# Adding residual rows and half of each attention output by accumulating transfers, and two gate tiles of their own, in a hybrid decoder block

## The chip, the cores and the metric

The kernel runs on one core of a Trainium2 chip. Its time is the device time of one execution in microseconds; the number that counts is the median of several executions. The core has TensorE (matrix products, written PE in the profile, its weight loads PEld), VectorE (DVE), ScalarE (ACT), GpSimd (POOL) and SyncE (SP). SP issues the transfers between DRAM and the on-chip memories.

## The reference

One decoder layer on x of 1024 rows by 1024 columns, all in float32, cut to what matters:

```
u = rmsnorm(x);  proj = u @ w_in                      # columns for both groups
ya = dilated_attention(q, k, v)                       # 8 heads x 64, causal, three dilated windows, merged softmax
yb = hgrn2(q, f, i): S_t = diag(f_t) S_(t-1) + (1 - f_t) i_t^T;  o_t = S_t^T q_t     # 4 heads x 128
yb = rmsnorm(o) * norm_w * silu(g)                    # g: the output gate
h  = x + concat(ya, yb) @ w_out                       # residual
h  = h + (silu(u2 @ w_gate) * (u2 @ w_up)) @ w_down,  u2 = rmsnorm(h)
out = rmsnorm(h)
```

## The kernel before

The whole kernel is a list of operations with costs, in program order, from which a scheduler in the kernel file writes out the order on each engine. `P.op` (and `P.flex`, for operations that may go to one of several engines) records an operation with its cost and the tiles that it reads and writes. `schedule` simulates the engines with these costs: an operation is ready when those that it depends on have ended, and among ready ones the class (`P.cls`, lower first) and then the longest remaining path decide. A transfer counts as landed 1.2 us after its issue (0.5 us), plus its bytes' time on a shared line (`moved`; 0.18 us for 64 KB), plus 0.97 us. At run time each engine takes its instructions in that order and waits on semaphores; it never passes a waiting instruction. Tiles are named by tag (`E0` to `E16`, `wh0`, `lm` and so on); a new tile with an old tag must wait until all uses of the old one have ended.

Matrix products are split in high and low float32r parts, three products for each; large ones use a Strassen scheme, so VectorE, ScalarE and POOL split, combine and evict.

The stages. First the input projection in twelve blocks of 256 or 512 columns; the last block is V. Its results go to DRAM (q_d, f_d, g_d, i_d, v_d and others). `hgrn(h)` runs the recurrence for heads 0 to 3 (class 0, the first to be picked), on the tiles E14 (f and the keys ks), E15 (q forms) and E16 (A, the score matrix, and iv, the values). It evicts scores to A on VectorE (lines 895 and 870), updates the state, forms o on TensorE from A and iv, normalises it and multiplies by the gate (line 958, recorded at L311 by `stt`). The gate g is loaded into A itself, `gt = A` (lines 945 and 946), after TensorE's last read of it. `attention(h, js)` (class 1) takes pairs of 128-row blocks: scores, masked maximum on VectorE (L1017, the mask `am` in E8), exponentials on ScalarE, scaling by the reciprocal (`wh<-wh,ri`) on POOL or VectorE, transposes (L1054), and the product with V. V is split in a high and a low part side by side in the weights, so the product has 128 rows: 64 of the high and 64 of the low part, which must be added. Two ScalarE copies (yb and ya in the tile `lm`), one add and one transfer bring 64 x 256 results to m_d in DRAM. The output projection (class 2, `out_proj`) fills TensorE's time in between: for each of eight row blocks t it first takes the recurrence rows 0 to 2 of the mixed matrix, later rows 3 to 7, and adds the product on VectorE to hn. hn starts as the rows of x, loaded beforehand into E13, E6, E15 and E16 by four transfers of 1 MB. Then come the norm, the gate/up products and the down product, in which TensorE is busy throughout.

Of the kernel before, what the change touches and what calls it, by code (L numbers as in the profile page):

```python
# [13 lines left out]
AF = mybir.ActivationFunctionType  # L14
OP = mybir.AluOpType
# [4 lines left out]
S = 1024  # L20
D = 1024
# [50 lines left out]
class Prog:  # L72
# [44 lines left out]
    class Clock:  # L117
# [7 lines left out]
        def to(self, t):  # L125
            while t >= (self.win + 1) * self.W:
                share = self.busy / self.W
                self.fast = share > 0.42 if self.fast else share > 0.84
                self.win, self.busy = self.win + 1, 0.0
# [123 lines left out]
def hymba_block(ctx: ExitStack, tc: tile.TileContext, x, norm1_w, w_in, lb_logits, hgrn_norm_w, w_out,  # L253
                norm2_w, w_gate_up, w_down, final_norm_w, cos, sin, amask, lmask, eye, out):
    nc = tc.nc
    x = x[0]
    out = out[0]
# [5 lines left out]
    P = Prog()  # L263
# [5 lines left out]
    def moved(nbytes, run):  # L269

        return nbytes / run * (0.008 + run / 27e3) / 16

    def dma(o, i, nbytes, run=2048):
        r = [i] if isinstance(i, (View, Buf)) else []
        w = [o] if isinstance(o, (View, Buf)) else []
        gi = i if r else (lambda: i)
        go = o if w else (lambda: o)
        P.op("SP", 0.5, lambda: nc.sync.dma_start(go(), gi()), r, w, nbytes=moved(nbytes, run))

    def mm(items, r, w):  # L280
        cost = sum(4 * n / 2400.0 + 0.008 if f32 else n / 2400.0 + (0.0132 if n > 128 else 0.007)
                   for o, lt, rh, st, sp, n, m, f32 in items)

        def fn():
            for o, lt, rh, st, sp, n, m, f32 in items:
                nc.tensor.matmul(o(), lt(), rh(), start=st, stop=sp, skip_group_check=True)  # L286
        P.op("PE", cost, fn, r, w)
# [9 lines left out]
    def bank_of(x):  # L297
        return (x.buf if isinstance(x, View) else x).pool == "ps"

    def two(n, psum=False):  # L300

        dve = ("DVE", 0.07 + n * 1.04e-3, not psum)
        return [dve] if psum else [dve, ("POOL", 0.17 + n * 2.1e-3, True)]

    def tt(eng, o, a, b, op, n, f=1.0):
        alts = two(n, bank_of(a) or bank_of(b) or bank_of(o) or op == OP.max)
        P.flex(alts, lambda e: ENG[e].tensor_tensor(o(), a(), b(), op=op), [a, b], [o])  # L307
# [16 lines left out]
    def act(o, a, func, n, scale=1.0, bias=None, accum=None):  # L324
        r, w, kw = [a], [o], {}
        cost = (0.06 if a.buf.pool == "ps" else 0.095) + n * 0.83e-3
        for k, s in (("scale", scale), ("bias", bias)):
            if isinstance(s, View):
                r.append(s)
                cost += 0.09  # L330
        if accum is not None:
            w.append(accum)
            cost += 0.09

        def fn():
            kw = {}
            if isinstance(scale, View) or scale != 1.0:
                kw["scale"] = scale() if isinstance(scale, View) else scale
            if bias is not None:
                kw["bias"] = bias()  # L340
            if accum is not None:
                kw["accum_out"] = accum()
            nc.scalar.activation(o(), a(), func, **kw)  # L343
        P.op("ACT", cost, fn, r, w, aset=SETS.get(func))
# [16 lines left out]
    whole = lambda b: b.v(lambda t: t)  # L361
# [9 lines left out]
    lm = P.buf("lm", [128, 10, 64], I32)  # L371
# [24 lines left out]
    def bank(stream, shape=(128, 512)):  # L396
        names = BANKS[stream]
        while True:
            n = rot[stream] = rot.get(stream, -1) + 1
            tag = f"b{names[n % len(names)]}"  # L400
            if tag not in held:
                return P.buf(tag, list(shape), F32, "ps")

    def turn(name, n):
        rot[name] = rot.get(name, -1) + 1
        return rot[name] % n
# [10 lines left out]
    def E(i, shape, dt=F32):  # L417
        return P.buf(f"E{i}", shape, dt)

    def colv(b, a, n, key):  # L420
        return b.v(lambda t: t[:, a:a + n], key)
# [10 lines left out]
    m_d = P.buf("m_d", [D, S], F32, "dr")  # L432
# [73 lines left out]
    def mm3(o, lh, ll, rh, rl, start, stop, n, m=128):  # L506
        return [(o, lh, rh, start, False, n, m, False), (o, lh, rl, False, False, n, m, False),
                (o, ll, rh, False, stop, n, m, False)]
# [321 lines left out]
    def hgrn(h):  # L830
        rs = slice(h * 128, h * 128 + 128)
        f, ks = colv(E14, 0, S, 0), colv(E14, S, S, 1)
        qp = colv(E15, 0, S, 0)
        A, iv = colv(E16, 0, S, 0), colv(E16, S, S, 1)
# [19 lines left out]
        def scores(n, g):  # L854

            ps = bank("h", (128, 2, 192))
            mm([(ps.v(lambda b, c=c: b[:, c, :n]), cs(ks, 2 * g + c),
                 E15.v(lambda t, c=c: t[:, S + (2 * g + c) * 192:S + (2 * g + c) * 192 + n]),
                 True, True, n, 128, True) for c in range(2)], [half(ks, g // 2), E15.v(None, 1)], [ps])
            return ps  # L860
# [31 lines left out]
        for g in range(4):  # L892
            ps = scores(192, g)
# [7 lines left out]
        for i, l in enumerate((1, 3, 5)):  # L901
# [8 lines left out]
            for g in range(4):  # L910
                ps = scores(192, g)
# [14 lines left out]
        for g in range(2):  # L926
            ps = bank("h")
# [9 lines left out]
        for c in range(NT):  # L937
            o = pj(po[c // 4], c % 4)
# [3 lines left out]
                it.append((o, cs(qp, c), cs(ks, c - 1), False, True, 128, 128, True))  # L942
                rd += [half(qp, c // 4), half(ks, (c - 1) // 4)]
            mm(it, rd, [o])
        gt = A
        dma(gt, g_d.v(lambda b: b[rs, :], h), 128 * S * 4)
        ss = P.buf("hss", [128, NT])
        for g in range(2):
# [10 lines left out]
            dma(m_d.v(lambda b, g=g: b[h * 128:h * 128 + 128, g * 512:g * 512 + 512], (h, g)), yg, 128 * 512 * 4)  # L959


    am = E(8, [128, 2048])
    ys = []
    amv = am.v(lambda t: t[:, :1920])
    EA = [[E(i, [128, 2048], F32R) for i in p] for p in ((9, 10), (11, 12))]
    probs = Ring(["wh4", "wh5", "wh6", "wh7", "wh8", "wh9", "wh10", "wh11"])
    PT = [("wl8", "wl9"), ("wl10", "wl11"), ("wl4", "wl5")]
# [19 lines left out]

    def attention(h, js):
        G = h // 4
        yb, ya = ys  # L990
        EQ, EV = EA[h % 2]
        qs, kh = colv(EQ, 0, S, 0), colv(EQ, S, S, 1)
        vv, kl = colv(EV, 0, S, 0), colv(EV, S, S, 1)
# [5 lines left out]
        for j in js:  # L999
            pr = {}  # L1000
            for b in (2 * j, 2 * j + 1):
                mx = None
                for g in range(b // 4 + 1):
                    n = min(512, (b + 1) * 128 - g * 512)
                    ps = bank("s")
# [6 lines left out]
                    p = probs()  # L1012
                    pn = p.buf.v(lambda t, p=p, n=n: p.get(t)[:, :n], p.key)
                    m = P.buf("mx%d" % turn("mx", 6), [128, 1])
                    o = 896 - b * 128 + g * 512
# [11 lines left out]
                for g in range(ng):  # L1027
                    p, pn, n = pr[b, g]
# [5 lines left out]
                for g in range(ng):  # L1034
                    p, pn, n = pr[b, g]
                    ts("POOL", pn, pn, whole(ri), 0.0, n)
            py = bank("y", (128, 256))
            for m2 in range(j + 1):
                diag = m2 == j
                n = 384 if diag else 512  # L1040
                pt = bank("t")
                many, col, rd = [], 0, set()
                for kb in (2 * m2, 2 * m2 + 1):
                    for b in (2 * j, 2 * j + 1):
                        if kb <= b:
                            p = pr[b, kb // 4][0]
# [22 lines left out]
                    it.append((py.v(lambda t, oc=oc: t[:, oc]), EV.v(lambda t, kb=kb: t[:, kb * 128:kb * 128 + 128], 0),  # L1069
                               tl.v(lambda t, cc=cc: t[:, cc]), False, last, nn, 128, False))  # L1070
                mm(it, [vh, vl, th, tl], [py])
            act(yb, py.v(lambda t: t[64:128, :]), AF.Copy, 256)
            act(ya, py.v(lambda t: t[:64, :]), AF.Copy, 256)
            tt("POOL", ya, ya, yb, OP.add, 256)
            dma(m_d.v(lambda b, j=j: b[512 + h * 64:576 + h * 64, j * 256:j * 256 + 256], (4 + h // 2, j // 2, h % 2, j % 2)), ya, 64 * 256 * 4, 1024)

    P.cls = 0
    for h in range(4):
        hgrn(h)
    P.cls = 1  # L1080
    yab = P.buf("lm", [64, 512])
    ys += [colv(yab, 256 * i, 256, i) for i in range(2)]
    dma(amv, amask, 128 * 1920 * 4)
    for h, js in [(h + i, js) for h in (0, 2, 4) for js in ((0, 1, 2), (3,)) for i in range(2)] + [
            (6, (0, 1)), (7, (0, 1)), (6, (2, 3)), (7, (2, 3))]:
        attention(h, js)
# [24 lines left out]
    def out_proj(t, *parts):  # L1111
        ht = hp[t]
        ks = [k for _, p, _ in parts for k in p]
        for n in range(2):
            ps = bank("o")
            for m, k, off in [(m, k, off) for m, p, off in parts for k in p]:
                lh, ll = (v.buf.v(lambda b, v=v, off=off: v.get(b)[:, off:off + 128]) for v in m[k])
                rh, rl = (v.buf.v(lambda b, v=v, n=n: v.get(b)[:, n * 512:n * 512 + 512], v.key) for v in WO[k])
                mm(mm3(whole(ps), lh, ll, rh, rl, k == ks[0], k == ks[-1], 512), [*m[k], *WO[k], *([before] if n else [])], [ps])
            before = ps  # L1120
            hn = ht.buf.v(lambda b, n=n: ht.get(b)[:, n * 512:n * 512 + 512], ht.key + (n,))
            tt("DVE", hn, whole(ps), hn, OP.add, 512)

    for k0 in (4, 6):
        wo(k0)
    for i in range(4):
        b = E((13, 6, 15, 16)[i], [128, 2, D])
        dma(b, x.rearrange("(t p) n -> p t n", p=128)[:, 2 * i:2 * i + 2, :], 1 << 20)
        for k in range(2):
            hp[2 * i + k] = b.v(lambda t, k=k: t[:, k, :], k)  # L1130
    for t in range(NT):
        if t in (5, 6):
            wo(0 if t == 5 else 2)
        out_proj(t, (mix(0, 3, t * 128, 128), (0, 1, 2), 0))
    for t in range(4):
        out_proj(t, (mix(3, 4, t * 128, 128), (3, 4, 5, 6), 0))
    ml = mix(7, 1, 0, 512)
    for t in range(4):
        out_proj(t, (ml, (7,), t * 128))
# [19 lines left out]
    for t in range(NT):  # L1159
        ht = hp[t]  # L1160
# [12 lines left out]
        if t >= 3 and len(leads) < LEAD:  # L1173
            p, up = gseq[len(leads)]
# [214 lines left out]
```

## Time and profile before

| | us |
|---|---|
| median of 3 executions | 1249.33 (1248.32 to 1254.5) |
| profiled execution, own time | 1252.68 |
| its span, first to last instruction | 1250.9 |
| TensorE busy | 1211.4 (97%) |
| VectorE busy | 1025.4 (82%) |
| ScalarE busy | 475.9 (38%) |
| POOL busy | 120.7 (10%) |

Times of day in the rows are microseconds from the start of the span. A matmul's end is modelled, so matmuls overlap in the rows and a busy TensorE is not always one at its peak. L286 is the line from which all matmuls are recorded, L307 all two-input operations (`tt`), L311 `stt`, L343 `act`, L353 and L355 the copies to the high part, L278 all transfers of `dma`. Transfers and waits on semaphores do not count as busy. Buffer numbers are left out: E is any of E0 to E16.

### The profile page before, as it was taken

The page shows a single profiled execution, that of the slowest core. Times are in us where ns is not written, and L with a number is a line of the kernel's source. Part 1 is how long each engine was busy: PE and PEld are TensorE (multiplying, and loading weights), DVE is VectorE, ACT ScalarE, POOL GpSimd, SP SyncE. Part 2 cuts the span into 40 slices and gives each one's busy share as a digit, 9 for nine tenths or more (in the row PEclk, how much of TensorE's full clock was granted, in tenths as well). Part 3 has the DMA queues.
Part 4 walks back from the last instruction along what each step waited for, and adds up shares of the span by engine and source line. Part 5 has one row for each costly group of instructions (what it writes and reads, how often), then busy time and mean ns, then how long its engine had stood idle before and what let it go on. Part 6 is the DMA issues. An engine that isn't in the chain of part 4 may idle for free.

```text
span 1250.9 us, 17947 instructions
## 1 busy us (share of the span) xinstructions
PE 1211.4 (97%) x6244; PEld 1032.8 (83%) x6244; DVE 1025.4 (82%) x2113; ACT 475.9 (38%) x1015; POOL 120.7 (10%) x216
## 2 busy tenths in 40 slices
PE   4999999999988999999999999999999999999997
PEld 4888889888988888987888888888888887888885
DVE  6999989998779999966888676676776769978986
ACT  5642332344326888841732132221222222223222
POOL 1110000101004454410100000000000000000001
PEclk9999999999989999999999999999999999999999
DMA  8334443514448753325223322323323369534433
GB/s 265 130 131 161 176 145 96 189 68 155 141 140 282 210 156 88 110 62 185 94 76 126 118 94 92 127 85 110 126 81 105 109 238 370 176 110 127 135 109 118
DMA packets 132522, 175.57 MB, mean 140 GB/s; under 512 B 18512, under 2 KB 85200, under 8 KB 132432
## 3 DMA queue, kind: packets, MB, share of 16 engines
q1 hardware_dynamic: 132432, 174.43, 42.7%
q8 instruction: 49, 0.80, 0.3%
q14 instruction: 41, 0.34, 0.1%
HBM read 122.76 MB, written 51.64 MB: 139 GB/s over the span
## 4 chain that ended last, share of the span: by engine, by line
PE 61%; DVE 4%; ACT 1%; issue 1%; POOL 1%; DMA 0%; DVEq 0%; POOLq 0%; ACTq 0%
PE b L286 59%; PE b L1054 2%; DVE E L307 1%; DVE wh L1017 1%; DVE wl L307 1%; ACT wh L343 0%; DMA m_d<-lm 0%; ACT wl L353 0%; PE b L292 0%; DVE E L311 0%; DVE lm L307 0%; ACT E L343 0%; DVE wh L320 0%; ACT lm L343 0%; ACT E L353 0%
## 5 line engine op out<-in xcount | busy, mean ns | idle before, releaser
L286 PE MATMUL b<-E,wh 128*128 128x512 f32 (+1 forms) x2096 | 643.3, 388 | 4.8 <-ACT wl L343 1.9
L286 PEld LDWEIGHTS b<-E,wh 128*128 128x128 f32 x2096 | 385.6, 188 | 82.7 <-DVE E L307 4.4
L286 PE MATMUL b<-E,wl 128*128 128x512 f32 (+1 forms) x1048 | 403.5, 385 | 0.0
L353 ACT ACTIVATE wh<-st 128x512 fp32r<-128x512 f32 (+1 forms) x203 | 127.1, 630 | 384.4 <-PE b L286 207.0
L307 DVE TENSOR_TENSOR wl<-st,wh 128x512 fp32r<-128x512 f32 x335 | 227.7, 690 | 6.8 <-ACT wh L353 3.5
L286 PEld LDWEIGHTS b<-E,wl 128*128 128x128 f32 x1048 | 197.1, 188 | 39.7
L307 DVE TENSOR_TENSOR E<-b,E 128x512 f32<-128x512 f32 (+1 forms) x157 | 105.9, 684 | 37.7 <-PE b L286 35.5
L355 DVE TENSOR_SCALAR wh<-st 128x512 fp32r<-128x512 f32 x125 | 52.8, 425 | 89.2 <-PE b L286 86.3
L286 PE MATMUL b<-wl,wh 128*128 128x512 f32 x308 | 119.9, 389 | 0.5 <-DVE wl L307 0.5
L286 PE MATMUL b<-wh,wl 128*128 128x512 f32 x308 | 119.9, 389 | 0.1
L286 PE MATMUL b<-wh,wh 128*128 128x512 f32 x308 | 119.8, 389 | 0.0
L286 PE MATMUL b<-wl,E 128*128 128x256 f32 (+1 forms) x544 | 115.9, 287 | 1.1 <-DVE wl L307 1.1
L286 PE MATMUL b<-E,E 128*128 128x192 f32 (+3 forms) x464 | 100.5, 327 | 4.5 <-DVE E L311 3.7
L307 DVE TENSOR_TENSOR wl<-b,wl 128x512 f32<-128x512 f32 (+2 forms) x139 | 89.8, 653 | 16.3 <-PE b L286 13.6
L307 DVE TENSOR_TENSOR st<-st 128x512 f32<-128x512 f32 x136 | 93.1, 689 | 0.7
L286 PEld LDWEIGHTS b<-wl,E 128*128 128x128 f32 x544 | 88.3, 192 | 4.3 <-DVE wl L307 1.5
L343 ACT ACTIVATE E<-E 128x512 f32<-128x512 f32 (+2 forms) x77 | 54.3, 706 | 97.6 <-DVE E L307 43.6
L286 PE MATMUL b<-wh,E 128*128 128x256 f32 x448 | 89.3, 291 | 0.1
L286 PEld LDWEIGHTS b<-E,E 128*128 128x128 f32 x464 | 76.1, 194 | 10.6 <-DVE E L311 3.9
L355 POOL TENSOR_SCALAR wh<-st 128x512 fp32r<-128x512 f32 (+1 forms) x15 | 10.2, 678 | 742.3 <-PE b L286 662.8
L286 PEld LDWEIGHTS b<-wh,E 128*128 128x128 f32 x448 | 72.6, 193 | 0.7 <-DVE wh L307 0.3
L286 PEld LDWEIGHTS b<-wl,wh 128*128 128x128 f32 x308 | 57.8, 188 | 13.0 <-DVE wl L307 1.0
(140 smaller groups left out, 1407.3 us busy)
## 6 DMA issues: line engine op xcount, KB each, us to landing
st<-in_w_gate_up_dram SPq DMA_DIRECT2D x22, 1024.0 KB, 5.2
st<-a_d SPq DMA_DIRECT2D x77, 256.0 KB, 3.0
st<-in_w_in_dram SPq DMA_DIRECT2D x16, 1024.0 KB, 5.6
a_d<-E SPq DMA_DIRECT2D x45, 256.0 KB, 2.2
E<-in_w_down_dram SPq DMA_DIRECT2D x44, 256.0 KB, 5.4
E<-in_x_dram SPq DMA_DIRECT2D x8, 512.0 KB, 9.1
E<-qs_d SPq DMA_DIRECT2D x32, 128.0 KB, 4.1
E<-kh_d SPq DMA_DIRECT2D x32, 128.0 KB, 4.1
```

Source lines behind the costliest of these rows:

```text
L286: nc.tensor.matmul(o(), lt(), rh(), start=st, stop=sp, skip_group_check=True)
L307: P.flex(alts, lambda e: ENG[e].tensor_tensor(o(), a(), b(), op=op), [a, b], [o])
L343: nc.scalar.activation(o(), a(), func, **kw)
L353: nc.scalar.activation(o(), i(), AF.Copy)
L355: ENG[e].tensor_scalar(o(), i(), 1.0, 0.0, op0=OP.mult, op1=OP.add)
L1017: nc.vector.tensor_tensor_reduce(pn(), pv(), am()[:, o:o + n], 1.0, -3e38 if mx is None else mx(), op0=OP.add, op1=OP.max, accum_out=m()),
L1054: nc.tensor.transpose(ov(), iv(), ident())
```

## The change

Three parts. The gate of head 2 is loaded to E8 and that of head 3 to f's half of E14, instead of to A; the mask `am` takes E8 only after the recurrence. An attention output is copied once, all 128 rows, to one of two tiles; SP transfers the first 64 rows to m_d, and POOL issues a second transfer that adds the other 64 rows to the same place in DRAM. And the first part of the output projection copies its product to hn, on ScalarE or VectorE, instead of adding it to x; then POOL issues a transfer that adds 128 rows of x to hn. The four loads of x for this are gone.

```
-        gt = A
+        gt = colv(E(8, [128, 2048]), 0, S, 0) if h == 2 else f if h == 3 else A
         dma(gt, g_d.v(lambda b: b[rs, :], h), 128 * S * 4)
...
-    am = E(8, [128, 2048])
     ys = []
-    amv = am.v(lambda t: t[:, :1920])
...
-        yb, ya = ys
...
-            act(yb, py.v(lambda t: t[64:128, :]), AF.Copy, 256)
-            act(ya, py.v(lambda t: t[:64, :]), AF.Copy, 256)
-            tt("POOL", ya, ya, yb, OP.add, 256)
-            dma(m_d.v(lambda b, j=j: b[512 + h * 64:576 + h * 64, j * 256:j * 256 + 256], (4 + h // 2, j // 2, h % 2, j % 2)), ya, 64 * 256 * 4, 1024)
+            y = ys[turn("y2", 2)]
+            act(y, whole(py), AF.Copy, 256)
+            to = m_d.v(lambda b, j=j: b[512 + h * 64:576 + h * 64, j * 256:j * 256 + 256], (4 + h // 2, j // 2, h % 2, j % 2))
+            dma(to, y.buf.v(lambda t, y=y: y.get(t)[:64, :], y.key), 64 * 256 * 4, 1024)
+            P.op("POOL", 0.9, lambda to=to, y=y: nc.gpsimd.dma_start(out=to(), in_=y.get(y.buf())[64:128, :], accum_op=OP.add),
+                 [y, to], [to], nbytes=moved(64 * 256 * 4, 1024))
...
-    yab = P.buf("lm", [64, 512])
+    yab = P.buf("lm", [128, 512])
     ys += [colv(yab, 256 * i, 256, i) for i in range(2)]
+    am = E(8, [128, 2048])
+    amv = am.v(lambda t: t[:, :1920])
     dma(amv, amask, 128 * 1920 * 4)
...
-            tt("DVE", hn, whole(ps), hn, OP.add, 512)
+            if 0 in ks:
+                P.flex([("ACT", 0.06 + 512 * 0.83e-3, False), ("DVE", 0.07 + 512 * 1.04e-3, False)], lambda e, o=hn, i=whole(ps):
+                       nc.scalar.activation(o(), i(), AF.Copy) if e == "ACT" else nc.vector.tensor_copy(o(), i()), [ps], [hn])
+            else:
+                tt("DVE", hn, whole(ps), hn, OP.add, 512)
+        if 0 in ks:
+            P.op("POOL", 0.9, lambda ht=ht, t=t: nc.gpsimd.dma_start(
+                out=ht(), in_=x[t * 128:t * 128 + 128, :], accum_op=OP.add), [ht], [ht], nbytes=moved(128 * D * 4, 4096))
...
-        dma(b, x.rearrange("(t p) n -> p t n", p=128)[:, 2 * i:2 * i + 2, :], 1 << 20)
```

## Rows read from the trace of the kernel before

**Rows 1.** The page: TensorE's total; the engines' shares of the chain.

```profile
PE 1211.4 (97%) x6244; PEld 1032.8 (83%) x6244; DVE 1025.4 (82%) x2113; ACT 475.9 (38%) x1015; POOL 120.7 (10%) x216
...
PE 61%; DVE 4%; ACT 1%; issue 1%; POOL 1%; DMA 0%; DVEq 0%; POOLq 0%; ACTq 0%
```

**Rows 2.** Stretches: length, busy us of five engines, granted clock, DMA share, GB/s.

```profile
345.00:350.00 5.00, 2.13 (x15) 1.87 (x15) 0.00 (x0) 0.76 (x3) 0.00 (x0) 0.96 1.02 287
350.00:355.00 5.00, 4.13 (x14) 4.13 (x15) 3.00 (x6) 0.00 (x0) 0.00 (x0) 0.50 0.75 282
...
400.00:405.00 5.00, 4.98 (x27) 4.84 (x28) 4.93 (x14) 4.56 (x15) 2.52 (x4) 0.66 0.60 182
...
410.00:560.00 150.00, 148.28 (x951) 131.02 (x949) 137.55 (x412) 115.79 (x308) 63.98 (x129) 1.00 0.45 126
```

**Rows 3.** Timeline of VectorE: start, duration, line, operation, idle before and its releaser.

```profile
350.07 0.75 DVE L311 SCALAR_TENSOR_TENSOR E<-b,hw,E 128x512 f32<-128x512 f32 x1 [6.76 <-DMA E<-g_d]
...
377.71 0.41 DVE L1017 CUSTOM_DVE_ANT_0 wh<-b,E 128x256 f32<-128x256 f32 x1
...
402.69 0.73 DVE L311 SCALAR_TENSOR_TENSOR E<-b,hw,E 128x512 f32<-128x512 f32 x1
```

**Rows 4.** Timeline of SP's queue: transfers by their issue.

```profile
334.82 0.36 SPq L278 DMA_DIRECT2D E<-in_amask_dram  x1
...
343.40 0.34 SPq L278 DMA_DIRECT2D E<-g_d  x1
...
393.81 0.57 SPq L278 DMA_DIRECT2D E<-g_d  x1
...
554.29 5.13 SPq L1104 DMA_DIRECT2D st<-m_d  x2
```

**Rows 5.** Timeline of TensorE around the two places.

```profile
345.91 0.82 PE L286 MATMUL b<-E,E 128*128 128x192 f32 x4
...
350.87 1.65 PE L286 MATMUL b<-E,E 128*128 128x192 f32 x4 [3.70 <-DVE E L311]
...
398.28 0.51 PE L286 MATMUL b<-E 128*128 128x512 f32 x1 [1.34 <-DVE mx L1017]
...
400.01 0.33 PE L286 MATMUL b<-E 128*128 128x128 f32 x1 [1.00 <-DVE mx L1017]
```

**Rows 6.** Transfers of the span: count, KB each, median us from issue to landing.

```profile
E<-in_x_dram SPq DMA_DIRECT2D x4, 1024.0 KB, 6.2
...
E<-g_d SPq DMA_DIRECT2D x4, 512.0 KB, 5.0
...
m_d<-lm SPq DMA_DIRECT2D x32, 64.0 KB, 2.6
...
E<-in_amask_dram SPq DMA_DIRECT2D x1, 960.0 KB, 8.1
```

**Rows 7.** Groups by shape from 405 to 550: busy, mean ns, idle before.

```profile
L307 DVE TENSOR_TENSOR E<-b,E 128x512 f32<-128x512 f32 x20 | 13.5, 676 | 2.0 <-PE b L286 1.7 <-issue 0.3
L307 DVE TENSOR_TENSOR lm<-lm 64x256 f32<-64x256 f32 x27 | 12.1, 447 | 0.4 <-ACT lm L343 0.3
...
L343 ACT ACTIVATE lm<-b 64x256 f32<-64x256 f32 x62 | 23.4, 377 | 7.0 <-DMA m_d<-lm 2.9 <-PE b L286 2.8 <-DVE lm L307 0.4
...
L307 POOL TENSOR_TENSOR wl<-st,wh 128x384 fp32r<-128x384 f32 x6 | 6.3, 1044 | 1.4 <-DVE wh L355 0.8 <-ACT wh L353 0.4
```

**Rows 8.** Waits of TensorE's weight loads, 410 to 560: total, times, longest.

```profile
PEld b L286 <- DVE mx L1017: 1.8, 3, 1.0
```

**Rows 9.** Transfers of attention outputs: issue ns min/median/max, first and last start.

```profile
L278 SPq DMA_DIRECT2D m_d<-lm x32: 445/451/543, 397.8 to 551.3; - x32
```

**Rows 10.** The chain that ended last, two of its pieces: start, duration.

```profile
461.08 5.33 DMA m_d<-lm
...
546.72 13.72 PE b L286 x66
```

## The prediction

> **What bounds the kernel now.** I read the totals first: TensorE is busy for 97% of the span and holds 61% of the chain that ended last, VectorE 4% [rows 1]. So a microsecond counts only where TensorE stands or runs slowly. I then cut the span into stretches of 5 us and looked for a low busy time or a granted clock under 1.00. Outside the first 30 us two places stand out. From 345 to 350 TensorE is busy 2.13 of 5.00 us and VectorE not at all, and the next 5 us run at a granted clock of 0.50, the 1.2 GHz level; 400 to 405 has a granted clock of 0.66 [rows 2]. From 410 to 560, the attention stage with output-projection work filled in, TensorE is busy 148.3 of 150 us, but VectorE 137.6 too [rows 2], so that stage has two engines near their limit and little to win.
>
> The timelines say who ends the waits. VectorE stands 6.76 us until the gate load of the third recurrence head lands; its gating multiply then starts at 350.07 [rows 3]. That load was issued at 343.40 [rows 4], since it writes over A, which TensorE was still reading. Behind the multiply in VectorE's queue is the eviction of the last head's scores, so TensorE stands 3.70 us, and its next four score matmuls take 1.65 us where four took 0.82 before [rows 5]. At 398.28 and 400.01 TensorE waits 1.34 and 1.00 us for the softmax maximum on VectorE [rows 5].
>
> **The gates in tiles of their own.** For head 2 the gate goes into E8, the tile that the mask takes before the change. The mask's load was issued at 334.82 [rows 4], so E8 was free by then, and the gate of head 2 can be loaded from there on, 8.6 us earlier. A gate load lands 5.0 us after issue in the median, the slowest price in sight is this one's 6.7 us (343.40 to 350.07) [rows 3, 4, 6]: it lands by 341.5 at the latest. The multiply is next bound by the transposes of the first half, whose following scores TensorE starts at 345.91 [rows 5], so it starts near 346 instead of 350. TensorE keeps its 3.70 us, and the time at half rate goes: 350.87 to 355.00 is 4.1 us, of which half, 2.1 us, was lost. Sum -5.8 us. Bounds: -3.7 if the clock falls all the same, -7 if the short waits around it close too. The work that fills the place is the V projection, which TensorE was still running between scores. What moves back is the mask: its load can start only after the second multiply, near 347, and lands 8.1 us later [rows 6], near 355; its first reader was at 377.71 [rows 3], some 6 us earlier after the change. 16 us of cover remain, so I cost it at nothing; without that cover it would delay all softmax work one for one.
>
> For head 3 the gate goes over f, which is free sooner than A. Its load was issued at 393.81 and its multiply, at 402.69, shows no wait before it [rows 3, 4]: 8.9 us lie between, against a landing of 5.0. Nothing to gain; the next writers of E14 are output weights loaded late in attention. Zero.
>
> **Attention outputs.** Each of 32 outputs loses one of two ScalarE copies (0.377 us each) and the add, nearly all on VectorE (0.447 us) [rows 7]; one copy over 128 rows has the same 256 columns, so 0.38. ScalarE sheds 12 us, VectorE 13. In their place POOL issues an accumulating transfer that must wait until the first transfer has landed.
>
> **Residual rows.** 16 adds on VectorE (0.676 us each [rows 7]) become copies that may go to ScalarE: up to 11 us off VectorE. Four loads of 1 MB [rows 6] leave SP's queue; eight accumulating transfers of 512 KB go to POOL's. Their readers, the later parts of the output projection, come tens of microseconds after, so a slow landing is covered.
>
> What the relief is worth: VectorE loses up to 24 of its 137.6 us. The waits it could shorten are 1.34 and 1.00 us, the slow clock of 400 to 405 (0.34 of 5 us, 1.7 us), and 1.8 us of weight loads waiting for the maximum from 410 to 560 [rows 2, 5, 8]: 5.8 us in all. Nothing is the lower end, all of it the upper. I take -2.5, under half, since the queue ahead of each maximum holds only one such add.
>
> The accumulating transfers have no row. Issuing a transfer takes SP 0.45 us [rows 9]; the nearest long POOL instruction takes 1.04 us [rows 7]. At 40 transfers this is 18 to 42 us on POOL, whose 64 us [rows 2] become at most 106 of 150: not a bound. I take the upper price, as the safe one. More dangerous is the wait. POOL runs in order; behind a transfer that waits stand the negated maximum, the sums and the scaling by the reciprocal, for which ScalarE's exponentials and TensorE's transposes wait. The first half lands after 2.6 us in the median [rows 6], but once 5.33 us lay on the chain [rows 10]. The kernel's own order allows 2.85 us from the start of an issue (0.5 + 1.2 + 0.18 + 0.97 in its code), so an ordinary landing costs nothing and a late one up to 2.5 us of POOL time. Lower end 0; upper end all 32 waits in full, 32 x 2.6 = 83 us, which takes POOL to 189 of 150 us and costs 39. I take +0.7, near the lower end because the order allows more than the median.
>
> The Trainium skill, DMA: Bandwidth & Descriptors (Anatomy of one DMA, and Two DMAs through the same engine are not ordered), states that DMA engines do not wait on semaphores: the issuing sequencer does, and a transfer that depends on another must wait for its completion. By that rule the wait of each accumulating transfer is POOL's own, and the cost may be anything up to that upper end; no row of this trace shows it, since POOL issues no transfer here.
>
> Buffers: an output buffer is now held for copy, landing, issue and second landing, 0.4 + 2.6 + 1.0 + 2.6 = 6.6 us, 9.3 with one landing of 5.33. There are two in turn, and 32 outputs come from 397.8 to 551.3 [rows 9], 4.8 us apart: 9.6 us for two. It just fits.
>
> The tail: the last output now reaches DRAM 1.0 + 2.6 - 0.4 = 3.2 us later, so the load of 554.29 [rows 4] moves to 557.5. TensorE has projection work of 13.72 us from 546.72 to 560.5 [rows 10], and the rows that do not need the last heads come first. Between 0 and +3.2; I take +0.6, as the load and split after it need about 5 us more.
>
> **Sum.** -5.8 - 2.5 + 0.7 + 0.6 = -7.0 us. The profiled execution's own time is 1252.68 (span 1250.9), 3.35 over the median of 1249.33; the same difference on the median gives 1242.3.
>
> **Rivals.** (1) The gate's stall goes, and the attention stage gives most of it back: late landings hold POOL. Five to eight outputs (an estimate: two for each fetch of a later pair of heads) that each cost TensorE 0.7 us return 3.5 to 5.6 us: 1245 to 1249. For it: the 5.33 us on the chain; against it: TensorE alone sets the chain in the second half of attention. (2) Slower: the accumulating transfer makes POOL the bound. POOL has 86 us free in 150; at 40 transfers it decides from 2.15 us each, issue and wait together. At 3 us each POOL has 184 us of work, 34 too many: about 1249 - 6 + 34 = 1277; at 2.5 us it is 1257. Against it: both rows near it lie under 1.1 us. (3) The ramp closes too: all 5.8 us of waits go, no cost beside: 1249.3 - 5.8 - 5.8 = 1238, with the gate's upper bound 1236. (4) The gate's load is late anyhow, because SP reaches it late behind the fetches of queries and keys: its stall stays and the rest is even, 1249. Against it: its tile is free 8.6 us before the old issue.
>
> **How the numbers follow.** Forecast 0.42, rival 1 0.30, rival 2 0.10, rival 3 0.14, rival 4 0.04. A measurement here tells 0.5%, 6.2 us, from no change, so faster means under 1243.1. The forecast's own range is 1239 to 1245 and lies mostly under that line: faster 0.37 + 0.14 = 0.51; same 0.05 + 0.30 + 0.04 = 0.39; slower 0.10. The range leaves out rival 2 and the far end of rival 3: 1236 to 1250.
>
> **What would show it.** Right: no wait for the gate before the multiply of head 2, a granted clock of 1.00 between 345 and 360, the mask issued after that multiply and no wait of the first softmax maximum for it. For attention: POOL's transfers near 1 us each, few waits that they end, ScalarE's copies halved to 32, the stage from 410 to 560 as long as before or 2 us shorter. Wrong: the wait for the gate in another place, VectorE or ScalarE waiting for POOL by more than now, POOL busy over 120 us in the stage, or a pause of TensorE near 555 to 565 that ends with the load of the last mixed rows.

## The result, and the profile after

| | us |
|---|---|
| changed kernel, median of 7 | 1258.12 (1257.52 to 1259.47) |
| kernel before, same occasions, median of 7 | 1251.31 (1248.32 to 1254.83) |
| ratio | 1.0055, 95% interval 1.0040 to 1.0071 |
| profiled execution: own time, span | 1257.52, 1255.7 |

The change makes the kernel about 7 us slower. The forecast was 1242.3 and the range ended at 1250. Every ratio below is to the kernel before, run on the same occasion; 0.001 of a ratio is taken as 1.25 us.

The page of the changed kernel: the totals, the transfers' queues (packets, MB, share of 16 engines), and the engines' shares of the chain that ended last.

```profile
PE 1208.2 (96%) x6244; PEld 1028.4 (82%) x6244; DVE 1022.0 (81%) x2107; ACT 464.7 (37%) x990; POOL 139.0 (11%) x223
...
q1 hardware_dynamic: 131344, 170.24, 41.2%
q0 software_dynamic: 3712, 6.29, 3.5%
...
PE 81%; DVE 8%; DMA 5%; issue 2%; ACT 1%; POOL 1%; SPq 1%; DVEq 0%; POOLq 0%; ACTq 0%
```

Against [rows 1], transfers have entered the chain: 0% before, 5% now. The stretches show where (columns as in [rows 2]):

```profile
345.00:350.00 5.00, 5.00 (x40) 4.93 (x39) 4.15 (x9) 0.69 (x1) 0.00 (x0) 1.00 0.59 163
350.00:355.00 5.00, 5.00 (x40) 5.00 (x39) 5.00 (x12) 1.58 (x2) 1.14 (x1) 1.00 0.71 243
...
510.00:515.00 5.00, 1.98 (x6) 1.80 (x7) 3.08 (x11) 2.28 (x6) 1.06 (x2) 0.78 0.78 171
...
410.00:550.00 140.00, 128.49 (x837) 113.36 (x836) 122.35 (x377) 98.81 (x264) 72.00 (x121) 0.99 0.71 156
```

The hole at 345 is closed: TensorE is busy 5.00 us where it was 2.13, and the clock is 1.00 where it was 0.50. The loss is in attention. The kernel before has in the same 140 us:

```profile
410.00:550.00 140.00, 138.28 (x907) 122.76 (x905) 133.71 (x406) 114.80 (x307) 63.98 (x129) 1.00 0.46 131
```

TensorE was busy 138.28 us before and is busy 128.49 us now, and the transfers' share rose from 0.46 to 0.71. VectorE and ScalarE are busy for less of this stretch too, partly because less work gets done in it: over the whole execution VectorE lost only 3.4 us (1025.4 to 1022.0) and ScalarE 11.2. TensorE no longer gets its operands in time. The waits from 410 to 550 (total, times, longest), first of TensorE, then of ScalarE before its copies of attention outputs and of POOL before its accumulating transfers:

```profile
PE b L286 <- DMA E<-kl_d: 5.0, 3, 3.2
PE b L1051 <- DVE wl L307: 3.6, 2, 1.9
PE b L286 <- ACT wl L353: 1.1, 1, 1.1
...
ACT lm L343 <- PE b L286: 11.8, 4, 4.3
ACT lm L343 <- PE b L1051: 1.3, 1, 1.3
...
POOL m_d L1073 <- DMA m_d<-lm: 13.1, 7, 3.7
```

Before, no wait of TensorE's matmuls in this stretch was over 0.7 us, and none was for keys. Two separate paths lead from the new transfers to TensorE.

**Late keys.** The timeline around the last fetch of keys: POOL's transfer, SP's issues, TensorE.

```profile
503.33 1.13 POOL L1129 DMA_DIRECT2D E<-in_x_dram  x1
...
504.03 3.20 SPq L278 DMA_DIRECT2D E<-kl_d  x4
...
513.02 0.45 PE L286 MATMUL b<-E,E 128*128 128x128 f32 x1 [3.16 <-DMA E<-kl_d]
```

The transfers issued from 499 to 516 (count, KB each, median us to landing), and the two queues there:

```profile
q1 hardware_dynamic: 2046, 2.84, 63.7%
q0 software_dynamic: 308, 0.66, 23.7%
...
E<-kl_d SPq DMA_DIRECT2D x5, 128.0 KB, 6.3
...
E<-in_x_dram POOLq DMA_DIRECT2D x1, 512.0 KB, 9.1
...
m_d<-lm POOLq DMA_DIRECT2D x3, 64.0 KB, 4.4
```

The same phase of the kernel before (498 to 515), with SP's issue of its last four loads of keys:

```profile
q1 hardware_dynamic: 2201, 3.08, 62.6%
...
E<-kl_d SPq DMA_DIRECT2D x7, 128.0 KB, 3.6
...
503.77 3.09 SPq L278 DMA_DIRECT2D E<-kl_d  x4
```

512 KB of residual rows were put in just ahead of the keys. The keys landed in 6.3 us instead of 3.6, TensorE stood 3.16 us, and its granted clock from 510 to 515 fell to 0.78. It is the landing that got longer, not the issue: SP took 3.20 us for the last four loads, and 3.09 us in the kernel before.

**Outputs held too long.** The second timeline, of POOL, ScalarE, VectorE and TensorE in order of time, shows the other path:

```profile
416.45 0.87 POOL L1073 DMA_DIRECT2D m_d<-lm  x1 [1.83 <-ACT lm L343]
...
423.57 0.38 ACT L343 ACTIVATE lm<-b 128x256 f32<-128x256 f32 x1 [3.23 <-PE b L286]
423.86 1.08 ACT L353 ACTIVATE wl<-b 128x512 fp32r<-128x512 f32 x2
...
424.48 0.69 DVE L307 TENSOR_TENSOR wl<-b,wl 128x512 fp32r<-128x512 f32 x1 [2.38 <-ACT wl L353]
...
425.23 0.66 PE L1051 MATMUL b<-ident,wh 128*128 128x128 f32 x4 [1.94 <-DVE wl L307]
```

The transfer issued at 416.45 landed 7.1 us later, at 423.55; ScalarE's copy into the place that it set free starts at 423.57. The trace puts this wait down to TensorE, but its product had been done since 420.8. Behind the copy on ScalarE stands the eviction that VectorE needs for the low part, which TensorE waits for. It happens again: the transfer of 459.19 landed after 8.6 us, at 467.8, the copy starts at 467.83, and TensorE stands 1.66 us at 470.07.

### The profile page after: what moved, and what is told of

Read it like the earlier page. It is cut to its first block, busy times and chain, and to the rows that moved or that the text cites. A ratio compares the mean times of both kernels' runs of the same rounds, so it can differ in the third digit from the quotient of the medians.

```text
span 1255.7 us, 17966 instructions
## 1 busy us (share of the span) xinstructions
PE 1208.2 (96%) x6244; PEld 1028.4 (82%) x6244; DVE 1022.0 (81%) x2107; ACT 464.7 (37%) x990; POOL 139.0 (11%) x223
## 3 DMA queue, kind: packets, MB, share of 16 engines
q0 software_dynamic: 3712, 6.29, 3.5%
## 4 chain that ended last, share of the span: by engine, by line
PE 81%; DVE 8%; DMA 5%; issue 2%; ACT 1%; POOL 1%; SPq 1%; DVEq 0%; POOLq 0%; ACTq 0%
PE b L286 78%; DVE E L307 2%; PE b L1051 2%; DVE wl L307 2%; DMA m_d<-lm 1%; DMA st<-in_w_in_dram 1%; PE b L292 1%; DVE E L870 1%; DVE wh L307 1%; SPq L278 1%; DMA E<-kl_d 0%; DVE E L882 0%; DVE E L879 0%; DMA st<-in_w_out_dram 0%; DMA st<-in_w_gate_up_dram 0%
## 5 line engine op out<-in xcount | busy, mean ns | idle before, releaser
L307 DVE TENSOR_TENSOR E<-b,E 128x512 f32<-128x512 f32 (+1 forms) x141 | 94.9, 683 | 39.5 <-PE b L286 37.1
```

## The experiments

### One part at a time: e1 to e4

The gates alone; gates and residual rows; gates and outputs; outputs alone. The gates' edit is the whole of e1:

```
-        gt = A
+        gt = colv(E(8, [128, 2048]), 0, S, 0) if h == 2 else f if h == 3 else A
...
-    am = E(8, [128, 2048])
     ys = []
-    amv = am.v(lambda t: t[:, :1920])
...
+    am = E(8, [128, 2048])
+    amv = am.v(lambda t: t[:, :1920])
```

e2 adds the hunks of `out_proj` and the dropped loads of x to this, e3 those of `attention` and `yab`; e4 is e3 without the edit above.

> The gate part alone; everything else as before. All theories: the wait of VectorE for the third head's gate and the 1.2 GHz stretch behind it go, as they did with the whole change, so 6 to 8 us faster than before, about 1244 us. If the whole change lost time through a moved mask or an unlucky order around the gates, this run shows it by being no faster.

> Gates and residual rows, attention outputs as before. Theory 1 (the accumulating transfers of the attention outputs lose the time, through POOL's wait and the later results): as fast as the gates alone, within 2 us. Theory 2 (the eight 512 KB accumulating transfers of x lose it, by delaying the loads of queries and keys): 6 us or more slower than the gates alone.

> Gates and attention outputs, residual rows as before. Theory 1: as slow as the whole change, 1255 to 1260. Theory 2: as fast as the gates alone, about 1244.

> Attention outputs alone. Theory 1: 8 to 13 us slower than before, 1260 or more, with more idle time of TensorE between 410 and 560. Theory 2: within 3 us of before.

| | median us | ratio | 95% interval |
|---|---|---|---|
| e1 gates | 1246.97 | 0.9966 | 0.9953 to 0.9978 |
| e2 gates, residual rows | 1259.03 | 1.0062 | 1.0050 to 1.0074 |
| e3 gates, outputs | 1253.35 | 1.0026 | 1.0011 to 1.0040 |
| e4 outputs | 1257.70 | 1.0052 | 1.0040 to 1.0064 |

The gates are a gain, 4.3 us alone and 3.3 on top of the outputs. Each of the other two parts turns it into a loss. So neither the residual rows nor the outputs explain the result by themselves; e3 and e4 came out between what the two theories had expected. But each of these kernels also has an order of its own, so the next runs keep one order.

### The transfers taken out, the order kept: e5, e6, e12, e8

The planner still counts the transfer, but nothing is issued. e5 has both edits on the changed kernel, e6 the second alone, e12 the first alone; e8 has the second on e2. Every other instruction stands where it stood.

```
-            P.op("POOL", 0.9, lambda to=to, y=y: nc.gpsimd.dma_start(out=to(), in_=y.get(y.buf())[64:128, :], accum_op=OP.add),
+            P.op("POOL", 0.9, lambda: None,
...
-            P.op("POOL", 0.9, lambda ht=ht, t=t: nc.gpsimd.dma_start(
-                out=ht(), in_=x[t * 128:t * 128 + 128, :], accum_op=OP.add), [ht], [ht], nbytes=moved(128 * D * 4, 4096))
+            P.op("POOL", 0.9, lambda: None, [ht], [ht], nbytes=moved(128 * D * 4, 4096))
```

> The changed kernel with its order of instructions kept, but none of the 40 accumulating transfers issued; left out: the residual and half of each attention output. Theory 1 (the transfers and the waits for them cost the time): as fast as the gates alone or up to 3 us faster, 1243 to 1248. Theory 3 (the new order of the other instructions costs it): still 1254 or more.

> The changed kernel with its order kept, without the eight accumulating transfers of x; left out: the residual. Theory 1a (these 512 KB transfers crowd out the loads of queries and keys): 5 to 9 us faster than the whole change, 1249 to 1253, and no wait of TensorE for keys. Theory 1b (the attention outputs' transfers are the cost): within 2 us of the whole change.

> The changed kernel, order kept, with the transfers of x but without the 32 accumulating transfers of the attention outputs; left out: half of each output. If the two kinds of transfers add up: 17 us less the 12 of x, so about 5 us faster than the whole change, 1253. If they hurt each other by sharing the DMA engines and POOL: clearly more, 1246 to 1250.

> Gates and residual rows with their order kept, without the eight transfers of x; left out: the residual. If the transfers cost the 12 us by which gates and residual rows are slower than the gates alone: 1244 to 1249. If the order does: still about 1258.

| changed kernel's order | median us | ratio | 95% interval |
|---|---|---|---|
| e5 neither kind issued | 1240.81 | 0.9911 | 0.9896 to 0.9927 |
| e6 outputs' transfers alone | 1245.77 | 0.9949 | 0.9930 to 0.9967 |
| e12 residual transfers alone | 1248.41 | 0.9975 | 0.9961 to 0.9989 |
| both (the changed kernel) | 1258.12 | 1.0055 | 1.0040 to 1.0071 |
| e8 (order of e2, none issued) | 1250.76 | 0.9992 | 0.9981 to 1.0002 |

The stretch 410 to 550 of e5, then e6, then e12:

```profile
410.00:550.00 140.00, 139.74 (x907) 124.81 (x906) 123.72 (x387) 100.03 (x268) 44.56 (x87) 1.00 0.43 119
```

```profile
410.00:550.00 140.00, 138.35 (x903) 122.68 (x903) 126.45 (x392) 104.00 (x275) 68.30 (x119) 1.00 0.57 140
```

```profile
410.00:550.00 140.00, 134.65 (x864) 119.33 (x863) 119.69 (x376) 97.38 (x262) 49.84 (x91) 0.99 0.59 142
```

Without its 40 accumulating transfers the changed kernel is 11 us faster than the kernel before; with them it is 7 us slower. They cost 18 us: residual rows alone 8.0, outputs alone 4.8, and 5.2 more together. (Four ratios with some 0.0016 each way make the last number uncertain by about 4 us.) With the residual transfers alone TensorE waits 4.4 us for keys and ScalarE's waits before its copies are the 4.1 us of e5; with the outputs' alone it waits 0.3 for keys, and ScalarE again 4.1. Only with both does ScalarE wait 13.3. TensorE's waits for keys in e6, then e12:

```profile
PE b L286 <- DMA E<-kl_d: 0.3, 1, 0.3
```

```profile
PE b L286 <- DMA E<-kl_d: 4.4, 3, 2.2
```

In e8 the transfers are worth 8.8 us of e2's excess, near the 8.0; the remaining 3.3 us over the gates alone are there without any transfer, in the new order with copies for adds.

TensorE runs the same 6244 matmuls in the same order in these kernels and in the changed one, so each matmul's start can be compared with its own in another trace (one execution of each). From 410 to 520 the changed kernel falls 15.3 us further behind e5; after that the distance hardly changes. Of the 15.3, 5.1 lie at two late fetches of keys (the matmuls at 502.99 and 513.02), 1.5 in the 4 us behind the second, at a granted clock of 0.60, and 3.9 at the two held outputs (before 425.23 and 470.07); the rest is spread over shorter waits. In the same way e12 falls 8.4 us behind e5: 5.0 at three late fetches of keys, 1.6 behind the last of them at a granted clock of 0.61, and 2.0 from 460 to 467, behind waits for ScalarE and VectorE. e6 falls 2.8 us behind, so 4.1 of the 15.3 come only with both.

### What a residual transfer costs: e9, e10

The changed kernel, order kept: e9 overwrites hn with x instead of adding (first edit); e10 adds 128 of the 1024 columns (second).

```
-                out=ht(), in_=x[t * 128:t * 128 + 128, :], accum_op=OP.add), [ht], [ht], nbytes=moved(128 * D * 4, 4096))
+                out=ht(), in_=x[t * 128:t * 128 + 128, :]), [ht], [ht], nbytes=moved(128 * D * 4, 4096))
```

```
-                out=ht(), in_=x[t * 128:t * 128 + 128, :], accum_op=OP.add), [ht], [ht], nbytes=moved(128 * D * 4, 4096))
+                out=ht()[:, 0:128], in_=x[t * 128:t * 128 + 128, 0:128], accum_op=OP.add), [ht], [ht], nbytes=moved(128 * D * 4, 4096))
```

> The changed kernel, order kept; POOL's eight 512 KB transfers of x overwrite the output rows instead of adding to them; left out: the product of the first part of the output projection. Same issue, same waits, same bytes from DRAM, no addition on the way. If the addition in the transfer is what costs (the DMA share rose more than the bytes): 1246 to 1250, near the run without these transfers. If their size, issue or wait is: 1255 to 1259.

> The changed kernel, order kept; the eight accumulating transfers take 128 of 1024 columns of x; left out: the residual in the other columns. Same issue and waits on POOL, an eighth of the traffic. If the traffic costs the 12 us: 1246 to 1249, DMA share between 410 and 550 near 0.59. If POOL's 1.1 us of issue each, or the wait, costs it: 1255 or more.

e9: 1253.00, ratio 1.0021 (1.0007 to 1.0035). e10: 1245.00, ratio 0.9948 (0.9933 to 0.9964), which is that of e6 with no residual transfer at all (0.9949). So issuing eight more transfers on POOL, with their waits, costs nothing that shows (give or take 3 us); the bytes do. Of the 13.3 us from e6 to the changed kernel, 9.0 are there when the rows are only copied and 4.3 (give or take 2.6) come with the addition, which here means all that the accumulating form brings: e9's expectation had the same issue, but its plain transfers also take POOL 0.71 us each (median) instead of 1.08. The waits of TensorE for keys follow: 5.0 us adding, 4.0 copying, 0.9 with an eighth of the bytes. The residual transfers (count, KB, median us to landing) of e9, then e10:

```profile
E<-in_x_dram POOLq DMA_DIRECT2D x8, 512.0 KB, 5.7
```

```profile
E<-in_x_dram POOLq DMA_DIRECT2D x8, 64.0 KB, 4.2
```

### What an output transfer costs: e7, e14

The changed kernel, order kept: e7 sends the second half plainly to a DRAM buffer of its own, so that it need not wait for the first (first edit); e14 sends it plainly over the first half, wait kept (second).

```
+    scr = P.buf("scr_d", [512, S], F32, "dr")
...
-            P.op("POOL", 0.9, lambda to=to, y=y: nc.gpsimd.dma_start(out=to(), in_=y.get(y.buf())[64:128, :], accum_op=OP.add),
+            P.op("POOL", 0.9, lambda h=h, j=j, y=y: nc.gpsimd.dma_start(
+                out=scr()[h * 64:h * 64 + 64, j * 256:j * 256 + 256], in_=y.get(y.buf())[64:128, :]),
```

```
-            P.op("POOL", 0.9, lambda to=to, y=y: nc.gpsimd.dma_start(out=to(), in_=y.get(y.buf())[64:128, :], accum_op=OP.add),
+            P.op("POOL", 0.9, lambda to=to, y=y: nc.gpsimd.dma_start(out=to(), in_=y.get(y.buf())[64:128, :]),
```

> The changed kernel with its order kept; the second half of each attention output goes to a DRAM buffer of its own by a plain transfer of POOL, which waits for nothing in DRAM; left out: half of each attention output in the mixed rows. Theory 1b by the wait (POOL held until the first half has landed): 4 to 8 us faster than the whole change, 1250 to 1254. If the issue on POOL and the traffic are the cost, within 2 us of the whole change.

> The changed kernel, order kept, but the second half of each attention output overwrites the first in DRAM instead of being added to it: the wait for the first half's landing, the issue and the bytes stay, only the addition goes; so the sums of the attention outputs are left out. Taking wait and addition away together (second half to a place of its own) gave back 8 us by the ratios. If the wait on POOL is the cost, the ratio stays near 1.0055 (1.0040 to 1.0070) and POOL's waits for the first half stay over 10 us. If the addition is the cost, the ratio falls to about 0.9993 (0.998 to 1.001) with the same waits in POOL's queue. Between the two it is shared.

e7: 1251.99, ratio 0.9993 (0.9976 to 1.0011). e14: 1253.09, ratio 1.0022 (1.0012 to 1.0031). From e12 without these transfers (0.9975) to the changed kernel (1.0055) there are 10.0 us: issue and bytes 2.3, waiting for the first half 3.6 more, the addition 4.1 more. Neither the wait nor the addition alone is the cost; each step is hardly larger than its uncertainty of about 2.5 us, their sum of 7.7 is. The addition here again stands for the whole accumulating form: in e14 an issue takes POOL 0.58 us (median) instead of 0.85, so not only the addition goes. POOL's waits for first halves in e14:

```profile
POOL m_d L1073 <- DMA m_d<-lm: 24.9, 10, 6.6
```

They are longer than the changed kernel's 13.1 us, and so are those of e9 (19.1) and e13 below (21.5), although all three are faster. How long POOL stands before these transfers does not by itself set the time. (These are the waits that the profile puts down to a landing; others before the same transfers it puts down to ScalarE and VectorE.)

### The planner's prices: e11

The planner counted the bytes of a residual transfer at 1.28 us of its shared line, those of an output at 0.18; e11 gives them 3.8 and 0.8 us, so that it plans around slower transfers, in a new order.

```
-                 [y, to], [to], nbytes=moved(64 * 256 * 4, 1024))
+                 [y, to], [to], nbytes=0.8)
...
-                out=ht(), in_=x[t * 128:t * 128 + 128, :], accum_op=OP.add), [ht], [ht], nbytes=moved(128 * D * 4, 4096))
+                out=ht(), in_=x[t * 128:t * 128 + 128, :], accum_op=OP.add), [ht], [ht], nbytes=3.8)
```

> The whole change, with the transfers' shares of the DMA line in the kernel's own planning raised to what the traces show (3.8 us instead of 1.28 for a row block of x, 0.8 instead of 0.18 for an attention output), so the order is new. If the loss is loads placed where the accumulating transfers hold the DMA engines, an order that knows it should win some of it back: 1248 to 1254. If the engines' time is simply missing, still 1256 to 1260.

1260.59, ratio 1.0072 (1.0057 to 1.0087): no better. The waits for keys are gone, but TensorE waits 6.1 us in eight places for low parts from VectorE. That the transfers only stood in the wrong places for want of a right price fell, in this form.

### A third place for the outputs: e13, e15

e13 rotates the outputs through three places but keeps the order (first edit); e15 tells the planner too (second).

```
-            y = ys[turn("y2", 2)]
+            y = (lambda o: colv(o.buf, 256 * turn("y3", 3), 256, o.key))(ys[turn("y2", 2)])
...
-    yab = P.buf("lm", [128, 512])
+    yab = P.buf("lm", [128, 768])
```

```
-            y = ys[turn("y2", 2)]
+            y = ys[turn("y2", 3)]
...
-    yab = P.buf("lm", [128, 512])
-    ys += [colv(yab, 256 * i, 256, i) for i in range(2)]
+    yab = P.buf("lm", [128, 768])
+    ys += [colv(yab, 256 * i, 256, i) for i in range(3)]
```

> The changed kernel, each engine's order kept, but the attention outputs rotate through three places of 128 x 256 instead of two. In the changed kernel two accumulating transfers landed 7.1 and 8.6 us after their issue, ScalarE's next copy to the tile started within 0.1 us of each landing, and the evictions behind it reached TensorE as waits for VectorE's low part (3.6 us in two). Theory of the tiles: with both kinds of transfer an output is held longer than two places allow, and this is the extra cost of having both (5 us): ScalarE's waits before the copy fall from 13.3 us to under 6, the 3.6 us on TensorE go, TensorE's waits for keys stay near 5 us, ratio to the kernel before 1.0015 (1.0000 to 1.0030). Rival, late keys alone: the places make no difference, ratio 1.0055 (1.0040 to 1.0070), TensorE waits elsewhere for as long.

> The changed kernel with three places for attention outputs that the planner knows of too, so the order differs. Theory of the tiles: about as in the run with the order kept, 1.000 to 1.003 of the kernel before. If the order as planned matters more than the tile, it lies anywhere from 0.998 to 1.008. Neither theory has it faster than the gates alone (0.9966).

e13: 1253.91, ratio 1.0028 (1.0016 to 1.0039). e15: 1261.28, ratio 1.0093 (1.0074 to 1.0111). Waits of e13 from 410 to 550, of ScalarE, TensorE and POOL:

```profile
ACT lm L343 <- PE b L286: 2.0, 2, 1.5
...
PE b L286 <- DMA E<-kl_d: 4.3, 3, 3.1
PE b L286 <- DVE wl L307: 2.3, 4, 1.4
...
POOL m_d L1073 <- DMA m_d<-lm: 21.5, 10, 5.0
```

ScalarE's 13.3 us before its copies become 2.0 and TensorE's two waits of 3.6 us are gone, while keys are as late as they were: the places were the second path. They give back 3.4 us (give or take 2.4) of the 5.2 that both kinds cost together, less than the 5 expected; part of it moved into other waits (2.3 us in four places). In an order planned for three places nothing is left of it.

## Why the prediction failed

**Gates: right in kind, the size near its lower end.** No wait for the gate, the multiply at 345.61 instead of 350.07, a clock of 1.00; the mask issued at 347.42 landed in 5.5 us and nobody waited for it. The forecast was -5.8; the profiled executions of e1 and before differ by 6.8 us, the medians by 3.9 (4.3 by the ratio). All lie in the bounds.

**Relief of VectorE and ScalarE: VectorE's part was mis-sized, and the gain is not shown by itself.** VectorE was to lose up to 24 of its 137.6 us. In e5, whose TensorE is as busy from 410 to 560 as before (148.6 us against 148.3), VectorE is busy 132.5 us: 5 less. The adds went, but the planner, which now has 40 issues at 0.9 us on POOL, gave VectorE other work. Its scalings by the reciprocal, before and in the changed kernel:

```profile
L320 DVE TENSOR_SCALAR wh<-wh,ri 128x512 f32<-128x512 f32 (+3 forms) x34 | 14.1, 428 | 0.3
```

```profile
L320 DVE TENSOR_SCALAR wh<-wh,ri 128x512 f32<-128x512 f32 (+3 forms) x46 | 23.0, 511 | 0.2
```

Of the waits that were to shorten, the 1.34 and 1.00 us of TensorE became three of 0.74, 1.08 and 0.80 us (390 to 397); but the granted clock behind them stayed at 1.00 where it was 0.66, and in e5 the weight loads' waits for the maximum fell from 1.8 to 0.2 us. By these rows some 3 us were won (an estimate), near the -2.5 taken. From e1 to e5 the time falls by 6.9 us (give or take 2.5), but this holds the new order and the four loads of x that are gone as well, and no run parts the three.

**Residual rows: the step that failed.** "Their readers ... come tens of microseconds after, so a slow landing is covered" costed 4 MB at nothing. Their own readers were indeed not late. But the step asked only who reads the transfer, not who shares the engines with it. The four loads of before were issued by 408.48, ahead of most of the attention stage; eight transfers in their place run from 412 to 524, beside fetches of queries and keys that TensorE needs soon: of those that SP began to issue at 504.03, the last held TensorE from 509.86 to 513.02. In e5's order they cost 8.0 us alone and 13.3 beside the outputs' transfers; e10 shows that it is their bytes.

**Attention outputs: the mechanism was named, the size was wrong.** +0.7 was taken for issue and late landings. Issue was well bounded: 0.85 us for an output and 1.08 for residual rows (medians) against 1.04 assumed, and POOL is busy 72.0 of 140 us. The outputs' cost was undersized: 4.8 us alone, 10.0 beside the residual rows. Their waits hold POOL for 13.1 us, but as e9, e13 and e14 show, the time does not follow this number; what e7 and e14 price by edits is 3.6 us for the wait and 4.1 for the addition. By the rule of the Trainium skill that the prediction weighed (DMA: Bandwidth & Descriptors, Anatomy of one DMA), the issuing sequencer waits; the trace agrees, since POOL's 13.1 us end with landings of first halves.

**"It just fits": failed.** An output was to be held 6.6 us, 9.3 at worst, against 9.6. Both of its terms took landings from a stage with a transfer share of 0.45 [rows 2]. With residual rows beside it the second landing alone took up to 8.6 us, as shown above; e13 prices this at 3.4 us (give or take 2.4).

**The addition itself had no price.** The sum treated an accumulating transfer as a plain one plus a wait. e9 and e14 price the addition at 4.3 and 4.1 us. The Trainium skill (DMA: Bandwidth & Descriptors, Rules for kernel authors) says that an accumulating transfer reads its destination and writes it later, which goes with this; no run here shows the read by itself.

**The rivals.** Rival 1 (stall gone, attention gives it back, late landings hold POOL) was the right kind, and its 3.5 to 5.6 us were a fifth to a third of the 18. Rival 2, the only one that ended slower, had the wrong mechanism: POOL is no bound, so that its 1257 us at 2.5 us for each transfer lies near the result is luck. Rivals 3 and 4 fell. The tail cost nothing: TensorE has no pause over 0.22 us from 553 to 570.

**The sum with measured terms.** -4.3 (gates) -6.9 (relief, order and the loads that are gone) +8.0 (residual rows) +4.8 (outputs) +5.2 (both together) = +6.8 us; these are differences of the ratios along one path of kernels, so they add up by construction. What is shown by an edit of its own is the bytes, the wait, the addition and the places. What stays open is how the 6.9 us divide, why the accumulating form costs what it does, and what e2 and e15 lose through their orders.

**The best version** is the first part alone, the gates: 1246.97, 0.9966 (0.9953 to 0.9978) of the time before, and faster than the changed kernel. e5, e6 and e10 are lower, but leave work out.

## What to carry to other kernels

Before moving work from an engine to transfers, read the transfers' share of the stage that they will run in and ask which loads there have the least slack, not only whether the new transfer's own reader can wait. A transfer that depends on another holds its issuing queue and its source buffer for two landings: size the rotation by the landing under the new load, not by the median of the old one. When a change replaces busy time that sits off the bound, test its gain and its cost apart in one fixed order; here -11 and +18 us stood behind a difference of 7. And where a planner chooses the engines, count the relief in its new plan: it filled much of VectorE's free time again.

## What the runs showed of the hardware

- From 499 to 516 the software queue moved 0.66 MB for 23.7% of 17 us on 16 engines and the hardware queue 2.84 MB for 63.7%: 6.1 and 3.8 us of all engines for a MB. From the kernel before, 498 to 515, it is 3.5 for the hardware queue. The packets differ (2.1 and 1.4 KB in the mean), so this is no price of one and the same packet.
- Over the whole execution the software queue moved the same 6.29 MB for 3.5% of the 16 engines' time in the changed kernel, for 2.7% in e9, where the residual rows do not add, and for 2.6% in e14, where the outputs do not. The 32 outputs went in 2560 packets when they added and in 1024 when they did not.
- Issuing an accumulating transfer took POOL 0.85 us for an output and 1.08 for residual rows, a plain one 0.58 (e14) and 0.71 (e9), all medians.
- An accumulating transfer of 512 KB into on-chip memory landed 7.0 us after issue in the median, a plain one from the same queue 5.7. Not all of this is the addition: without the outputs' transfers beside them the accumulating ones landed in 6.2 (e12). One of 64 KB to DRAM landed in 2.9 in the median and 8.6 at most; without residual transfers beside it the longest was 5.5 (e6).
